# Attention's value step: sums' transposes behind the products, both ScalarE copies together, the latent keys' copy on ScalarE

## The chip, the cores and the metric

The kernel runs on one core of one Trainium2 chip. The metric is the device time of an execution in microseconds. TensorE multiplies and transposes into PSUM, VectorE, ScalarE and GpSimd do the rest, and SyncE mostly issues DMAs. Each engine works through its own queue in order and waits for the others by semaphores.

## The reference, cut to what matters

An encoder trunk of two layers over 1024 tokens of 1024 columns. A layer has a mixer with three groups of heads (6 gated DeltaNet heads, 6 grouped-query attention heads, 4 latent-attention heads), an output projection, and a mixture of experts. The change lies in the attention of the two softmax groups, 10 heads per layer, and in the keys of the latent one:

```python
def attend(q_blk):
    s = jnp.einsum('bhgqd,bhkd->bhgqk', q_blk, k) * scale
    p = jax.nn.softmax(s, axis=-1)
    return jnp.einsum('bhgqk,bhkd->bhgqd', p.astype(v.dtype), v)
...
kv = (rms_norm(ckv, kv_lat_gain) @ w_ukv).reshape(B, S, H, MLA_NOPE + MLA_V)
k_nope = rms_norm(kv[..., :MLA_NOPE], kn_gain)
v = kv[..., MLA_NOPE:]
```

## The kernel before

A layer runs in stages: input projection and the DeltaNet chunks' preparation, then one long attention stage (`attend`) into which the DeltaNet scan, the making of the latent heads' inputs (`mla_inputs`), the modulation products for later (`ada`) and the loading of the output weights are mixed, then output projection, routing and experts. Everything is written out in Python; a scheduler orders the instructions of each engine afterwards, so that the written order is only a start: a change of a few lines moves the neighbours too.

`attend` goes through 10 heads with 8 query blocks of 128 tokens. For a block, `scores` multiplies queries and keys into two PSUM tiles `s` of 128x512, VectorE takes the maximum (L1132, L1134), ScalarE the exponential with its row sums (L1137). At every second block VectorE adds the two halves of the row sums (L1142, tile `rs`, 128x2) and takes the reciprocal (L1143). `trans` transposes the probabilities on TensorE (L1157) and copies them to `pT`, one half on ScalarE (L1162), the other on VectorE (L1160).

`values` closes a pair of blocks; there are 80 such pairs in the two layers. It takes the one PSUM tile `pv` (a whole bank, one buffer) for two things. TensorE first spreads the reciprocals over 64 partitions by two transposes (L1171, into `rsb`, partitions 0 to 63), then does eight products (L1175) that fill partitions 0 to 63 with the even and 64 to 127 with the odd key tiles. ScalarE copies the odd half to `olo` (L1178), VectorE adds both halves to `o` (L1179), ScalarE copies `rsb` (L1182) to another buffer of the name `olo`, which has two, and GpSimd multiplies (L1183). The result goes to DRAM by a DMA on ScalarE's queue (L1186). The next pair's transposes have to wait until `pv` has been read.

In `mla_inputs`, `products` makes the latent heads' rows, 16 times in the two layers: a product of 128x512 in a PSUM tile `pt` holds keys and values of four heads. VectorE copies the keys to `mK` (L584), ScalarE the values to `mV` (L585), both out of this one tile.

GpSimd works all through the stage, for `ada` (L123, L125), for the scan and for the DeltaNet output (L917, L930).

Of the kernel before, what the change touches and what calls it, by code (L numbers as in the profile page):

```python
# [8 lines left out]
FT = mybir.dt.float32  # L9
FR = mybir.dt.float32r  # L10
I32 = mybir.dt.int32
AF = mybir.ActivationFunctionType
OP = mybir.AluOpType
# [16 lines left out]
class Trunk:  # L30
# [497 lines left out]
    def mla_inputs(self, l, mx, tp, wk):  # L528

        nc, I = self.nc, self.I  # L530
# [38 lines left out]
        def products(lat, t, Q, K, V):  # L569
            ps = self.pt_p.tile([128, 4, 128], FT, name="pt")  # L570
            nc.tensor.transpose(ps[:, 0, :], lat[:, t, 0:128], self.ident)
            nc.tensor.transpose(ps[0:64, 1, :], lat[:, t, 128:192], self.ident)
            nc.tensor.transpose(ps[:, 2, :], lat[:, t, 192:320], self.ident)
            ct = wk.tile([128, 3, 128], FT, name="ct")
            for j, n in ((0, 128), (1, 64), (2, 128)):
                nc.scalar.activation(ct[0:n, j, :], ps[0:n, j, :], AF.Copy, scale=gq[0:n, j:j + 1])
            yield
            pq = self.pt_p.tile([128, 4, 128], FT, name="pt")
            pqv = pq.rearrange("p a b -> p (a b)")[:, 0:384]
            self._prod(nc, pqv, [(ct[:, 0, :], wuq[:, 0, :]), (ct[0:64, 1, :], wuq[0:64, 1, :])])  # L580
            nc.scalar.activation(Q[:, t].rearrange("p a b -> p (a b)"), pqv, AF.Copy)
            pk = self.pt_p.tile([128, 4, 128], FT, name="pt")
            nc.tensor.matmul(pk.rearrange("p a b -> p (a b)"), ct[:, 2, :], wukv, start=True, stop=True)
            nc.vector.tensor_copy(K[:, t, :, 0:64], pk[:, :, 0:64])  # L584
            nc.scalar.activation(V[:, t], pk[:, :, 64:128], AF.Copy)  # L585

        lat = latent(0)
# [1 line left out]
        for c in range(4):  # L589
# [4 lines left out]
            K = wk.tile([128, hn, 4, 96], FT, name="mK", bufs=self.QB)  # L594
# [4 lines left out]
            for _ in products(cur, 0, Q, K, V):  # L599
                yield  # L600
            if c < 3:
                lat = latent(c + 1)
            for _ in products(cur, 1, Q, K, V):
                yield
# [490 lines left out]
    def attend(self, mx, heads, aside):  # L1095
        nc = self.nc
        seq = [(hd, qt) for hd in heads for qt in range(NT)]
        ops, gens, P, PT = {}, {}, {}, {}
        self.dn_done, self.att_over, turn = False, False, {"s": 0, "p": 0, "v": 0}

        def bank(which):

            if self.dn_done:
                turn[which] += 1
                if turn[which] % self.TM[which] in self.TB[which]:
                    return self.dps.tile([128, 512], FT, name="dn")
            return {"s": self.s_p, "p": self.pt_p, "v": self.pv_p}[which].tile([128, 512], FT, name={"s": "s", "p": "pt", "v": "pv"}[which])

        def scores(u):
            (h, prep, row, scale), qt = seq[u]  # L1110
            if u == 0:
                gens[h] = prep()
                next(gens[h])
                ops[h] = next(gens[h])
            if u // NT + 1 < len(heads):
                h1, p1 = heads[u // NT + 1][:2]
                if qt == 0:
                    gens[h1] = p1()
                    next(gens[h1])
                if qt == self.QP:  # L1120
                    ops[h1] = next(gens[h1])
            passes = ops[h][0]
            i = u % 2
            if i == 0:
                self.su = self.wp.tile([128, 4], FT, name="su", bufs=3)
            su = self.su
            sm = self.wp.tile([128, 4], FT, name="sm", bufs=6)
            ss = []
            for kf in range(2):
                s = bank("s")  # L1130
                self._prod(nc, s, [(q[:, qt * 128:qt * 128 + 128], k[:, kf * 512:kf * 512 + 512]) for q, k in passes])
                nc.vector.tensor_reduce(sm[:, kf:kf + 1], s, axis=AX.X, op=OP.max)  # L1132
                ss.append(s)
            nc.vector.tensor_scalar(sm[:, 2:3], sm[:, 0:1], sm[:, 1:2], -scale, op0=OP.max, op1=OP.mult)  # L1134
            p = self.wp.tile([128, NT, 128], FT, name="P", bufs=self.PB)
            for kf in range(2):
                nc.scalar.activation(p[:, 4 * kf:4 * kf + 4].rearrange("p a b -> p (a b)"), ss[kf], AF.Exp, bias=sm[:, 2:3], scale=scale,  # L1137
                                     accum_out=su[:, 2 * kf + i:2 * kf + i + 1])
            rs = None
            if i:  # L1140
                rs = self.wp.tile([128, 2], FT, name="rs", bufs=3)
                nc.vector.tensor_tensor(rs, su[:, 0:2], su[:, 2:4], op=OP.add)  # L1142
                nc.vector.reciprocal(rs, rs)  # L1143
            P[u] = p, rs

        def trans(u):
            p, rs = P.pop(u)
            i = u % 2
            if i == 0:
                PT[u // 2] = (self.wp.tile([128, NT, 256], FT, name="pT"),)  # L1150
            pT = PT[u // 2][0]
            if i:
                PT[u // 2] += (rs,)
            for hf in range(2):
                ps = bank("p").rearrange("p (a b) -> p a b", a=4)
                for k in range(4):
                    nc.tensor.transpose(ps[:, k, :], p[:, hf * 4 + k, :], self.ident)  # L1157
                o = (slice(None), slice(hf * 4, hf * 4 + 4), slice(i * 128, i * 128 + 128))
                if hf:
                    nc.vector.tensor_copy(pT[o], ps)  # L1160
                else:
                    nc.scalar.activation(pT[o], ps, AF.Copy)  # L1162

        def values(w):
            (h, _, row, _), qt = seq[2 * w]
            V = ops[h][1]
            pT, rs = PT.pop(w)
            both = bank("v").rearrange("p (a b) -> p a b", a=2)
            pv, rsb = both[:, 0], both[0:64, 1]
            for i in range(2):  # L1170
                nc.tensor.transpose(rsb[:, i * 128:i * 128 + 128], rs[:, i:i + 1].to_broadcast([128, 64]), self.ident)  # L1171

            for k in range(NT):
                hs = slice(64 * (k % 2), 64 * (k % 2) + 64)
                self.pe_last = nc.tensor.matmul(pv[hs], V[:, k, :], pT[:, k, :], start=(k < 2), stop=(k >= NT - 2), tile_position=(0, hs.start))  # L1175
            o = self.wp.tile([64, 256], FT, name="o")
            lo = self.wp.tile([64, 256], FT, name="olo")
            nc.scalar.activation(lo, pv[64:128], AF.Copy)  # L1178
            nc.vector.tensor_tensor(o, pv[0:64], lo, op=OP.add)  # L1179
            if self.OM:  # L1180
                rr = self.wp.tile([64, 256], FT, name="olo")
                nc.scalar.activation(rr, rsb, AF.Copy)  # L1182
                nc.gpsimd.tensor_tensor(o, o, rr, op=OP.mult)  # L1183
            else:
                nc.vector.tensor_tensor(o, o, rsb, op=OP.mult)
            self.qa.dma_start(mx["oT"][qt // 2][row:row + 64], o)  # L1186

        n = len(seq)
        la = self.LA
        for u in range(la):  # L1190
            scores(u)
        for u in range(n):
            if self.VF and (u - self.VL) % 2 == 0 and u >= self.VL + 1:
                values((u - self.VL - 1) // 2)
            if u + la < n:
                scores(u + la)
            trans(u)
            if not self.VF and (u - self.VL) % 2 == 1 and u >= self.VL + 1:
                values((u - self.VL - 1) // 2)
            next(aside, None)  # L1200
        for w in sorted(PT):
            values(w)
        self.att_over = True
        for _ in aside:
            pass
        self.pe_last = None
# [678 lines left out]
```

## Time and profile before

| | |
|---|---|
| median of 3 runs | 2909.56 us (2903.85 to 2910.96) |
| the profiled execution's own time | 2897.23 us |
| its span, first to last instruction | 2895.4 us |
| mean granted clock of TensorE | 0.911 of full |
| TensorE, VectorE, ScalarE, GpSimd busy | 2443.4, 1971.0, 1365.3, 1414.9 us |
| attention stage of layer 0 | about 438 to 960 us |
| attention stage of layer 1 | about 1866 to 2356 us |

The profile is of one execution. Its rows name engines PE (TensorE), PEld (its weight load), DVE (VectorE), ACT (ScalarE), POOL (GpSimd) and SP (SyncE). A row's "x80" counts instructions, three numbers behind it are the shortest, the median and the longest in ns, and "waits" are idle times of an engine with the instruction that ended them.

### The profile page before, as it was taken

To read this page: it belongs to the slowest core of one execution; us is meant where nothing else is said; L and a number is where in the kernel's file an instruction comes from. 1 tells how busy PE (TensorE), PEld (TensorE's weight loads), DVE (VectorE), ACT (ScalarE), POOL (GpSimd) and SP (SyncE) were. 2 spreads that over 40 slices of the span, in tenths; PEclk is the share of its full clock that TensorE was granted. 3 is DMA by queue.
4 is the path that set the end of the run, shared out by engine and by line. 5 is a ranking of instruction groups with operands and counts; after the bars stand their busy time and mean duration, and the time that the engine had idled before them with its cause. 6 is when DMAs were issued, how large, how long until landed. Compare 5 with 4: busy or idle time off the path is not lost. (4 is left out here: it accounts for less than half of the span.)

```text
span 2895.4 us, 46986 instructions
## 1 busy us (share of the span) xinstructions
PE 2443.4 (84%) x16804; PEld 1834.1 (63%) x16804; DVE 1971.0 (68%) x3424; ACT 1365.3 (47%) x2500; POOL 1414.9 (49%) x1425
## 2 busy tenths in 40 slices
PE   4978976988699968999959879779888999699986
PEld 4866864656467856765548768646565678566543
DVE  5596779587777467676625867795967754866654
ACT  4436335654466225455454263356565742345543
POOL 2874766455667233234337837663656412332432
PEclk9989978999799979999969889889998999799988
DMA  7435653686454647999754356537784445599994
GB/s 236 124 91 141 163 141 89 178 210 169 116 154 117 230 176 252 304 308 324 254 131 126 91 141 158 137 90 184 205 201 116 122 144 189 198 311 290 313 321 140
DMA packets 499532, 534.51 MB, mean 185 GB/s; under 512 B 252722, under 2 KB 421234, under 8 KB 490592
## 3 DMA queue, kind: packets, MB, share of 16 engines
q1 hardware_dynamic: 397408, 461.93, 52.4%
q0 software_dynamic: 19680, 33.61, 5.4%
q10 hardware_dynamic: 82208, 35.93, 4.9%
q8 instruction: 134, 2.20, 0.3%
q14 instruction: 102, 0.84, 0.1%
HBM read 436.03 MB, written 124.65 MB: 194 GB/s over the span
## 5 line engine op out<-in xcount | busy, mean ns | idle before, releaser
L1579 DVE TENSOR_TENSOR wlo<-w,whi 128x2048 fp32r<-128x2048 f32 x126 | 287.7, 2289 | 88.0 <-ACT whi L1576 82.8
L1576 ACT ACTIVATE whi<-w 128x2048 fp32r<-128x2048 f32 x130 | 247.6, 1911 | 118.7 <-PE up L219 99.4
L1137 ACT ACTIVATE P<-s,sm 128x512 f32<-128x512 f32 x294 | 199.2, 683 | 101.7 <-DVE sm L1134 58.3
L1132 DVE TENSOR_REDUCE sm<-s 128x1 f32<-128x512 f32 x294 | 198.5, 682 | 57.5 <-PE s L219 55.5
L123 POOL TENSOR_TENSOR ada_wt<-ada_wt,cs 128x512 f32<-128x512 f32 (+1 forms) x128 | 187.0, 1464 | 101.2 <-DMA ada_wt<-in_ada_w 100.0
L125 POOL TENSOR_TENSOR ada_wt<-ada_wt 128x256 f32<-128x256 f32 (+2 forms) x256 | 209.5, 826 | 5.4
L219 PE MATMUL acc<-whi,hhi 128*128 128x280 f32 x640 | 194.7, 315 | 10.0 <-ACT hhi L193 5.3
L1157 PE MATMUL pt<-ident,P 128*128 128x128 f32 x1136 | 181.4, 295 | 25.8 <-DVE qh L996 7.8
L219 PE MATMUL acc<-whi,hlo 128*128 128x280 f32 x640 | 198.7, 314 | 3.2 <-POOL hlo L196 3.2
L219 PE MATMUL acc<-wlo,hhi 128*128 128x280 f32 x640 | 195.6, 309 | 0.3 <-DVE wlo L212 0.2
L1175 PE MATMUL pv<-pT,vr 128*64 128x256 f32 x1280 | 184.5, 410 | 8.7 <-DVE pT L1160 5.5
L219 PE MATMUL s<-kh,qh 128*128 128x512 f32 (+1 forms) x294 | 148.1, 504 | 47.3 <-ACT P L1137 45.5
L1157 PEld LDWEIGHTS pt<-ident,P 128*128 128x128 f32 x1136 | 143.1, 151 | 66.5 <-issue 10.9
L1631 POOL DMA_INDIRECT xg<-xn,itok x75 | 112.2, 1496 | 149.3 <-PE xt L1647 99.5
L219 PE MATMUL y<-w,aT 128*128 128x512 f32 x360 | 166.9, 603 | 0.5 <-ACT aT L1683 0.5
L219 PE MATMUL up<-whi,hTh 128*128 128x512 f32 x360 | 152.8, 426 | 0.5 <-ACT hTh L1648 0.5
L219 PE MATMUL up<-wlo,hTh 128*128 128x512 f32 x360 | 146.0, 406 | 6.4 <-DVE wlo L1579 6.4
L219 PE MATMUL up<-whi,hTl 128*128 128x512 f32 x360 | 148.7, 413 | 0.0
L1183 POOL TENSOR_TENSOR o<-o,olo 64x256 f32<-64x256 f32 x80 | 59.2, 740 | 173.7 <-ACT olo L1182 158.2
L1175 PEld LDWEIGHTS pv<-pT,vr 128*64 128x64 f32 x1280 | 88.2, 144 | 77.4 <-issue 37.0
L219 PEld LDWEIGHTS acc<-whi,hhi 128*128 128x128 f32 x640 | 125.5, 200 | 17.3 <-ACT hhi L193 6.1
L219 PEld LDWEIGHTS acc<-whi,hlo 128*128 128x128 f32 x640 | 127.1, 199 | 9.3 <-POOL hlo L196 4.1
(480 smaller groups left out, 6901.3 us busy)
## 6 DMA issues: line engine op xcount, KB each, us to landing
w<-in_moe_w SPq DMA_DIRECT2D x260, 512.0 KB
w<-in_moe_w SPq DMA_DIRECT2D x65, 1024.0 KB
ada_wt<-in_ada_w SPq DMA_DIRECT2D x96, 256.0 KB
dg<-ch SPq DMA_DIRECT2D x64, 288.0 KB
ada_wt<-in_ada_w SPq DMA_DIRECT2D x32, 512.0 KB
ch<-aq SPq DMA_DIRECT2D x64, 192.0 KB
wraw<-in_w_in SPq DMA_DIRECT2D x32, 280.0 KB
qkr<-gqk ACTq DMA_DIRECT2D x32, 256.0 KB
```

Source lines behind the costliest of these rows:

```text
L123: eng.tensor_tensor(wt, wt, self.cs.unsqueeze(2).to_broadcast([128, KT, cols]), op=OP.mult)
L125: eng.tensor_tensor(wt[:, 0:n, :], wt[:, 0:n, :], wt[:, n:2 * n, :], op=OP.add)
L219: mm = nc.tensor.matmul(ps, a, b, start=(i == 0), stop=(i == n - 1))
L1132: nc.vector.tensor_reduce(sm[:, kf:kf + 1], s, axis=AX.X, op=OP.max)
L1137: nc.scalar.activation(p[:, 4 * kf:4 * kf + 4].rearrange("p a b -> p (a b)"), ss[kf], AF.Exp, bias=sm[:, 2:3], scale=scale, accum_out=su[: ...
L1157: nc.tensor.transpose(ps[:, k, :], p[:, hf * 4 + k, :], self.ident)
L1175: self.pe_last = nc.tensor.matmul(pv[hs], V[:, k, :], pT[:, k, :], start=(k < 2), stop=(k >= NT - 2), tile_position=(0, hs.start))
L1183: nc.gpsimd.tensor_tensor(o, o, rr, op=OP.mult)
L1576: c = nc.scalar.activation(hi, w, AF.Copy)
L1579: s = (nc.gpsimd if first is not None and first < self.HB - 1 else nc.vector).tensor_tensor(lo, w, hi.bitcast(FT), op=OP.subtract)
L1631: nc.gpsimd.indirect_dma_start(out=g[0:n], out_offset=None, in_=st["xn"], in_offset=bass.IndirectOffsetOnAxis(ap=it[0:n], axis=0), bounds_ ...
```

## The change

In `values` the two transposes of the reciprocals stand behind the eight products. ScalarE's two copies stand together, behind the products and ahead of VectorE's sum, and the second one has a tile name of its own, `orr`, with two buffers. GpSimd's multiplication is as before; the branch for a switch that was always on is gone. In `products` ScalarE copies the keys too. Behind the change L1173 are the products, L1175 the transposes, L1180 and L1181 the copies, L1182 the sum; L1183 is the multiplication in both.

```diff
@@ -581,7 +581,7 @@
             nc.scalar.activation(Q[:, t].rearrange("p a b -> p (a b)"), pqv, AF.Copy)
             pk = self.pt_p.tile([128, 4, 128], FT, name="pt")
             nc.tensor.matmul(pk.rearrange("p a b -> p (a b)"), ct[:, 2, :], wukv, start=True, stop=True)
-            nc.vector.tensor_copy(K[:, t, :, 0:64], pk[:, :, 0:64])
+            nc.scalar.activation(K[:, t, :, 0:64], pk[:, :, 0:64], AF.Copy)
             nc.scalar.activation(V[:, t], pk[:, :, 64:128], AF.Copy)
 
         lat = latent(0)
@@ -1167,22 +1167,20 @@
             pT, rs = PT.pop(w)
             both = bank("v").rearrange("p (a b) -> p a b", a=2)
             pv, rsb = both[:, 0], both[0:64, 1]
-            for i in range(2):
-                nc.tensor.transpose(rsb[:, i * 128:i * 128 + 128], rs[:, i:i + 1].to_broadcast([128, 64]), self.ident)
 
             for k in range(NT):
                 hs = slice(64 * (k % 2), 64 * (k % 2) + 64)
                 self.pe_last = nc.tensor.matmul(pv[hs], V[:, k, :], pT[:, k, :], start=(k < 2), stop=(k >= NT - 2), tile_position=(0, hs.start))
+            for i in range(2):
+                nc.tensor.transpose(rsb[:, i * 128:i * 128 + 128], rs[:, i:i + 1].to_broadcast([128, 64]), self.ident)
+
             o = self.wp.tile([64, 256], FT, name="o")
             lo = self.wp.tile([64, 256], FT, name="olo")
+            rr = self.wp.tile([64, 256], FT, name="orr")
             nc.scalar.activation(lo, pv[64:128], AF.Copy)
+            nc.scalar.activation(rr, rsb, AF.Copy)
             nc.vector.tensor_tensor(o, pv[0:64], lo, op=OP.add)
-            if self.OM:
-                rr = self.wp.tile([64, 256], FT, name="olo")
-                nc.scalar.activation(rr, rsb, AF.Copy)
-                nc.gpsimd.tensor_tensor(o, o, rr, op=OP.mult)
-            else:
-                nc.vector.tensor_tensor(o, o, rsb, op=OP.mult)
+            nc.gpsimd.tensor_tensor(o, o, rr, op=OP.mult)
             self.qa.dma_start(mx["oT"][qt // 2][row:row + 64], o)
 
         n = len(seq)
```

**ScalarE, layer 0, the first value step of the stage.** The words in brackets are the engines whose semaphores an instruction waits for; `gsq` and `lat` belong to the latent rows. Before:

```order
L1178 ACTIVATE olo<-pv 64x256 [waits PE_49]
L559 ACTIVATE gsq<-lat 128x704 [waits DMAHW6_49,DVE_49,Activation_49]
L1162 ACTIVATE pT<-pt 128x4x128 [waits PE_49]
L1182 ACTIVATE olo<-pv 64x256 [waits DVE_49]
L1137 ACTIVATE P,su<-s,sm 128x512 [waits DVE_49]
L1137 ACTIVATE P,su<-s,sm 128x512
```

With the change:

```order
L1180 ACTIVATE olo<-pv 64x256 [waits PE_49]
L1181 ACTIVATE orr<-pv 64x256
L559 ACTIVATE gsq<-lat 128x704 [waits DMAHW6_49,DVE_49,Activation_49]
L1162 ACTIVATE pT<-pt 128x4x128 [waits PE_49]
L1137 ACTIVATE P,su<-s,sm 128x512 [waits DVE_49]
L1137 ACTIVATE P,su<-s,sm 128x512
```

The second copy waits for VectorE no more and follows the first; so it is at all 80 pairs.

**ScalarE, layer 0, one of the 16 latent products.** `mQ`, `mK` and `mV` are the latent queries, keys and values, `x` belongs to the scan. Before:

```order
L883 ACTIVATE x<-dn 64x384 [waits DMAHW1_49,PE_49]
L1178 ACTIVATE olo<-pv 64x256 [waits PE_49]
L1182 ACTIVATE olo<-pv 64x256 [waits DVE_49]
L581 ACTIVATE mQ<-pt 128x384 [waits PE_49]
L1186 DMA oT_134<-o 64x256 [waits DMAHW0_49,Pool_49]
L585 ACTIVATE mV<-pt 128x256 [waits DVE_49]
L1137 ACTIVATE P,su<-s,sm 128x512 [waits Activation_49]
```

With the change:

```order
L883 ACTIVATE x<-dn 64x384 [waits PE_49]
L1184 DMA oT_134<-o 64x256 [waits DMAHW4_49,Pool_49]
L581 ACTIVATE mQ<-pt 128x384 [waits PE_49]
L584 ACTIVATE mK<-pt 128x4x64 [waits PE_49]
L585 ACTIVATE mV<-pt 128x256
L1137 ACTIVATE P,su<-s,sm 128x512 [waits DVE_49,Activation_49]
```

Keys and values are now copied one after the other with a wait for TensorE alone, and the value step's copies have gone elsewhere in the queue.

**TensorE, layer 0, the second value step.** `s` are scores, the products with `qkr` are the next head's transposes. Before:

```order
L1171 MATMUL pv<-ident,rs 64x128 x2
L1175 MATMUL pv<-pT,vr 64x256
L219 MATMUL s<-kh,qh 128x512
L219 MATMUL s<-kl,qh 128x512
L1175 MATMUL pv<-pT,vr 64x256 x3
L219 MATMUL s<-kh,qh 128x512
L219 MATMUL s<-kl,qh 128x512
L991 MATMUL pt<-ident,qkr 128x128 x4
L1175 MATMUL pv<-pT,vr 64x256 x4
L1157 MATMUL pt<-ident,P 128x128 x8
```

With the change:

```order
L1173 MATMUL pv<-pT,vr 64x256 x3
L219 MATMUL s<-kh,qh 128x512
L219 MATMUL s<-kl,qh 128x512
L1173 MATMUL pv<-pT,vr 64x256
L219 MATMUL s<-kh,qh 128x512
L219 MATMUL s<-kl,qh 128x512
L991 MATMUL pt<-ident,qkr 128x128 x4
L1173 MATMUL pv<-pT,vr 64x256 x4
L1175 MATMUL pv<-ident,rs 64x128 x2
L1157 MATMUL pt<-ident,P 128x128 x8
```

The transposes of the reciprocals went from the head of the step to its end; in between, the products are cut in other places by scores.

## Rows read from the trace of the kernel before

**Rows 1.** The page's part 1: busy time, share of the span and instructions of each engine.

```profile
PE 2443.4 (84%) x16804; PEld 1834.1 (63%) x16804; DVE 1971.0 (68%) x3424; ACT 1365.3 (47%) x2500; POOL 1414.9 (49%) x1425
```

**Rows 2.** Busy time in two attention stages; columns: stretch, length, then engines' busy time (instructions).

```profile
438.00:960.00 522.00, 436.23 (x3914) 309.77 (x3914) 381.57 (x783) 287.14 (x681) 302.04 (x332) 0.90 0.56 150
1866.00:2356.00 490.00, 414.82 (x3898) 296.84 (x3898) 365.90 (x799) 289.47 (x686) 247.98 (x294) 0.92 0.57 150
```

**Rows 3.** Who waits around tile olo (us, times): first the waiters for it, then reverse.

```profile
L1179 DVE TENSOR_TENSOR o<-pv,olo x80: 381/414/419, 454.1 to 2354.0; 64x256 f32<-64x256 f32 x80
L1182 ACT ACTIVATE olo<-pv x80: 358/377/379, 454.6 to 2354.5; 64x256 f32<-64x256 f32 x80
...
  ACT olo L1182: 158.2, 42
  DVE o L1179: 49.8, 33
...
  ACT olo L1178: 37.0, 22
...
  PE pv L1171: 14.6, 10
```

**Rows 4.** Line L585, ScalarE's copy of V, and tile mK's copy L584 on VectorE.

```profile
L585 ACT ACTIVATE mV<-pt x16: 378/383/384, 563.1 to 2104.7; 128x256 f32<-128x256 f32 x16
...
  DVE mK L584: 29.1, 13
...
L584 DVE COPY mK<-pt x16: 407/424/426, 562.6 to 2104.2; 128x256 f32<-128x256 f32 x16
```

**Rows 5.** Busy time in 46 stretches of ScalarE's waits at L1182 and L585, the sum.

```profile
sum 78.97, PE 52.11 PEld 35.41 DVE 75.58 ACT 0.13 POOL 52.65; mean PE 1.13 PEld 0.77 DVE 1.64 ACT 0.00 POOL 1.14
```

**Rows 6.** Timeline from 747 us; columns: start, length, engine, line, operation, idle before it.

```profile
747.38 3.86 POOL L917 TENSOR_TENSOR os<-os,ob 128x384 f32<-128x384 f32 x4
747.39 8.25 DVE L1142 TENSOR_TENSOR rs<-su 128x2 f32<-128x2 f32 x1 [0.92 <-ACT P L1137]
...
751.88 3.75 POOL L123 TENSOR_TENSOR ada_wt<-ada_wt,cs 128x1024 f32<-128x1024 f32 x2
```

**Rows 7.** The same view, 838 to 848 us.

```profile
838.17 7.49 DVE L1142 TENSOR_TENSOR rs<-su 128x2 f32<-128x2 f32 x1
...
846.36 0.41 DVE L1179 TENSOR_TENSOR o<-pv,olo 64x256 f32<-64x256 f32 x1
...
846.80 0.38 ACT L1182 ACTIVATE olo<-pv 64x256 f32<-64x256 f32 x1 [4.56 <-DVE o L1179]
...
847.23 0.44 PE L1171 MATMUL pv<-ident,rs 128*64 128x128 f32 x2 [1.61 <-ACT olo L1182]
```

**Rows 8.** Who waits for the reciprocals, tile rs; the addition L1142 in it.

```profile
L1142 DVE TENSOR_TENSOR rs<-su x80: 130/160/8248, 447.7 to 2344.7; 128x2 f32<-128x2 f32 x80
...
  PE pv L1171: 16.1, 6
```

**Rows 9.** Timeline, 2194 to 2218 us.

```profile
2194.17 1.08 PE L1175 MATMUL pv<-pT,vr 128*64 128x256 f32 x8
...
2215.91 0.38 ACT L1182 ACTIVATE olo<-pv 64x256 f32<-64x256 f32 x1 [5.17 <-DVE o L1179]
...
2216.99 0.20 DVE L1134 TENSOR_SCALAR sm<-sm 128x1 f32<-128x1 f32 x1
2217.22 0.69 ACT L1137 ACTIVATE P<-s,sm 128x512 f32<-128x512 f32 x1 [0.19 <-DVE sm L1134]
...
2218.06 0.79 PE L219 MATMUL s<-kh,qh 96*128 96x512 f32 x1 [6.66 <-ACT P L1137]
```

**Rows 10.** The addition L1142 in layer 0's attention stage, then in layer 1's.

```profile
L1142 DVE TENSOR_TENSOR rs<-su 128x2 f32<-128x2 f32 x40 | 40.0, 1000 | 15.4 <-ACT P L1137 15.2
...
L1142 DVE TENSOR_TENSOR rs<-su 128x2 f32<-128x2 f32 x40 | 11.7, 293 | 15.8 <-ACT P L1137 15.6
```

## The prediction

> **What bounds the kernel now.** I read the page first: TensorE is busy for 84% of the span, VectorE for 68%, ScalarE for 47% [rows 1]. No engine is the bound of the whole, so I asked for each engine's busy time by stage. The change touches only the two attention stages, 438 to 960 us and 1866 to 2356 us, 1012 us together [rows 2]. There TensorE is busy for 436.23 + 414.82 = 851.05 us and idle for 161 us; VectorE is busy for 747.47 us, 0.74 of the time; ScalarE for 576.6 us, 0.57. The reader should see that nobody is full there: the stages are a ring of queues kept in order (scores, maximum, exponential, transposes, copies, value products), and time is lost where the queues meet.
>
> The third view is the wait lists of the instructions that the change touches. ScalarE's copy of the sums' part (L1182) kept its engine idle for 49.8 us, 33 times, until VectorE's sum L1179 was done [rows 3], though it needs no number from it. In the latent part the copy of V (L585) waited 29.1 us, 13 times, for VectorE's copy of K out of the same PSUM tile [rows 4]. So ScalarE stands still for 78.97 us in 46 stretches because VectorE is late.
>
> The fourth view decides how much of that is worth anything: each engine's busy time in those 46 stretches, summed [rows 5]. Of the 78.97 us, VectorE is busy for 75.58 (96%) and TensorE for 52.11. So VectorE isn't waiting for ScalarE there, it is what everybody waits for, and TensorE idles in 26.9 us of it.
>
> The fifth view, the timeline, says why VectorE is late. At 747.39 the sum of two row sums (L1142, 128x2, median 160 ns) takes 8.25 us, from GpSimd's first product at 747.38 until the pair of products that begins at 751.88 has ended at 755.63; at 838.17 it takes 7.49 us, and ScalarE's stall of 4.56 us before 846.80 is its tail [rows 6, 7]. All 80 of these take 40.0 + 11.7 = 51.7 us [rows 10] instead of 80 x 0.16 = 12.8 [rows 8], so some 39 us go into them.
>
> **The change part by part.** The sum is made against the profiled execution, 2897.23 us (span 2895.4 us and 1.8 around it). The median of the runs shown is 2909.56, 12.33 above it (0.4%); I take that offset over.
>
> (a) *K's copy moves to ScalarE.* VectorE loses 16 copies of 0.42 us, 6.7 us [rows 4]. Weighted with its busy share in the stages that is 6.7 x 0.74 = 5.0 us. ScalarE gains 16 copies; the same shape for V takes 0.383 us there [rows 4], so 6.1 us, on an engine idle for 435 us of the 1012, which also loses the 29.1 us of stalls: nothing. Should ScalarE be the late engine where a head's latents are made, the 6.1 us would stand on the path.
>
> (b) *ScalarE no longer stops for VectorE.* All 96 waits are gone from the order. The gain lies between nothing and the 26.9 us in which TensorE idled in the stalls. I take a tenth, 2.7 us, because the row that shows a whole case shows next to none: after the stall of 5.17 us before 2215.91 the exponential starts at 2217.22, right behind the maximum that VectorE ends at 2217.19, and TensorE's wait of 6.66 us ends with that exponential [rows 9]. Without the stall the exponential could not have started earlier.
>
> (c) *The bank is freed one step earlier.* The products' tile has one PSUM buffer. TensorE's next value step waited 14.6 us, 10 times, for L1182, its last reader [rows 3]. At 847.23 it starts 0.41 us after the sum's end at 846.77 [rows 7]. Now the sum is the last reader: 10 x 0.41 = 4.1 us.
>
> (d) *The transposes go behind the products.* They need the reciprocal of the row sums, and TensorE waited 16.1 us for it, 6 times, with the products queued behind [rows 8]. Now the products go first. The gain lies between 0 and 16.1 us. I take the first four of eight products, half of 1.08 us [rows 9], at each of the 6: 3.2 us, since products five to eight need VectorE's own half of the transposed probabilities, which is late when the reciprocal is. The transposes cost the same as before; the products end 0.38 us earlier for it, so the first copy doesn't start later.
>
> (e) *The sum now comes behind both copies.* VectorE waited 37.0 us, 22 times, for the first copy [rows 3]; each such wait grows by the second copy, 0.377 us: 22 x 0.37 = 8.1 us, weighted 0.74: 6.0 us lost. Below: nothing, if the sum's place in the queue moves as well. Above: both copy and transposes at full price, 22 x 0.75 = 16.5 us. Behind a waiting sum stand maxima and copies of probabilities, and ScalarE's exponentials wait for those. The wait itself follows from the rows: L1182 stood waiting for a sum that it shares only the bank with, so the reverse order waits as well. [...] Were only data waited for, (e) would be nought and the sum 15.0 us of gain.
>
> (f) *A tile of its own for the reciprocals* costs 2 KB a partition and takes one tie to GpSimd's multiplication away. GpSimd's waits for L1182 (158.2 us) [rows 3] become waits for the sum, 0.41 us earlier; the output's DMA follows the multiplication as before. Nothing. No transfer is added or taken away on any queue; the scheduler shifts them with their neighbours.
>
> Sum: -5.0 - 2.7 - 4.1 - 3.2 + 6.0 = **-9.0 us**, that is 2888.2 for the profiled execution and 2909.56 - 9.0 = **2900.6** for the median.
>
> **The rivals.**
>
> *VectorE stays late and nothing else counts.* Then ScalarE's stall only moves to its next wait for VectorE's maximum; (b), (c) and (d) fall away and -5.0 + 6.0 = +1.0 us remain: **2910.6**. For it speak the 96% of rows 5 and the case of rows 9; against it that TensorE's waits in (c) and (d) are its own, with products ready.
>
> *A worse meeting with GpSimd.* The change re-sorts every queue in the two stages, and so the moments at which L1142 meets a train of GpSimd products. Mechanism: an addition that starts just as such a train starts waits for its end, and maximum and copies wait behind it. Price: the same 40 additions took 40.0 us in layer 0 and 11.7 in layer 1 [rows 10]. If layer 1 comes to look like layer 0, VectorE loses 28.3 us, weighted 0.74: 20.9, and -9.0 + 20.9 = +11.9 us: **2921.5**. It decides from 9.0/0.74 = 12.2 us more in L1142. [...]
>
> *The ring turns freely.* If TensorE gets back all it idled in the stalls, -26.9 - 5.0 - 4.1 + 6.0 = -30.0 us: **2879.6**. The meeting of the rival before, the other way round, gives nearly the same (-9.0 - 20.9). For it: 161 us of TensorE's idle time and 79 us of a wait without need. Against: rows 5.
>
> *It doesn't do what it says.* The order shows both copies together without a wait between at all 80 places, so 1 in 50; **2909.6**.
>
> **How the numbers follow.** A measurement of this kernel can tell about 0.3%, 8.7 us, from no change. Chances: my forecast 0.36, VectorE late 0.27, worse meeting 0.19, free ring 0.16, nothing done 0.02. The forecast itself lies close to the bound: of its 0.36, 0.26 go to faster, 0.08 to same, 0.02 to slower. VectorE late: 0.02, 0.21, 0.04. Worse meeting: 0, 0.03, 0.16. Free ring: all faster; nothing done: same. Together 0.44 faster, 0.34 same, 0.22 slower. The low end takes TensorE's 26.9 us and VectorE's 6.7 us whole and charges nothing: 2876.0. The high end takes (e) at its upper bound with nothing gained, 16.5 us: 2926.1; the four times worked out lie inside.
>
> **What would show it.** In the profile after: ScalarE's waits for the sum and for K's copy gone (79 us to 0); VectorE's wait in front of the sum up from 37 us to some 45; the wait for the reciprocal gone from in front of the value step and no equal wait for transposed probabilities in its place; TensorE idle in the two stages down from 161 us by about 9. If L1142 adds up to far more or less than 51.7 us, the meeting with GpSimd has decided. I am wrong if TensorE's idle time in the two stages doesn't fall, or if the stages outside them change by more than the attention stages do.

## The result, and the profile after

The changed kernel takes **2873.68 us** (median of 6 executions, 2861.89 to 2886.54); the kernel before took 2902.47 in the same session (2896.19 to 2910.96). The ratio is **0.9898, interval 0.9865 to 0.9931**: the medians lie 28.8 us apart. The same changed kernel, measured a second time, gave 2882.81 against 2896.96, 14.2 us apart, ratio 0.9936 [0.9906, 0.9966]. (A ratio here can differ from the quotient of the two medians, in this case 0.995, by some 0.2%.) Forecast were -9.0 us and a range down to 2876.0; of the 26.9 us between the forecast 2900.6 and 2873.68, 7.1 are the kernel before's own median, which was 2909.56 when the forecast was made.

The profiled execution of the changed kernel took 2886.54 us (span 2884.7), the slowest of its six, while the one of before was near its fastest. So the two traces differ by 10.7 us, not 28.8, and I profiled each kernel once more. The seven lines below are the changed kernel's stages in the view of stretches (columns as in [rows 2]): layer 0's attention, its output projection, its experts, layer 1's preparation, then layer 1's attention, output projection and experts.

```profile
435.90:918.10 482.20, 404.96 (x3843) 291.44 (x3840) 366.80 (x767) 285.85 (x684) 292.26 (x323) 0.92 0.58 151
918.10:1040.50 122.40, 113.29 (x572) 96.38 (x571) 50.19 (x63) 28.44 (x48) 31.77 (x18) 0.92 0.61 202
1040.50:1457.10 416.60, 354.13 (x1505) 229.42 (x1505) 279.98 (x344) 187.56 (x221) 136.44 (x95) 0.91 0.84 271
1457.10:1857.30 400.20, 341.75 (x2469) 297.82 (x2471) 275.45 (x504) 177.29 (x301) 268.14 (x309) 0.87 0.53 138
1857.30:2345.60 488.30, 407.63 (x3806) 290.05 (x3803) 353.17 (x763) 286.80 (x684) 230.77 (x266) 0.91 0.52 135
2345.60:2449.70 104.10, 102.30 (x546) 87.68 (x544) 48.87 (x63) 28.24 (x48) 22.37 (x8) 0.99 0.66 223
2449.70:2884.70 435.00, 368.03 (x1546) 240.32 (x1546) 286.75 (x347) 189.60 (x221) 164.02 (x97) 0.91 0.81 262
```

The same view of the kernel before, its stages cut at the same instructions:

```profile
438.60:947.30 508.70, 422.93 (x3848) 298.73 (x3845) 376.87 (x776) 283.51 (x676) 300.82 (x331) 0.90 0.55 145
947.30:1056.00 108.70, 106.70 (x572) 91.39 (x570) 49.10 (x64) 28.23 (x48) 22.40 (x10) 1.00 0.65 218
1056.00:1475.70 419.70, 355.40 (x1504) 231.12 (x1504) 280.72 (x343) 187.84 (x222) 141.21 (x95) 0.90 0.82 269
1475.70:1887.60 411.90, 342.38 (x2467) 298.02 (x2469) 277.09 (x504) 179.70 (x302) 271.30 (x308) 0.87 0.52 134
1887.60:2354.90 467.30, 401.74 (x3807) 286.55 (x3804) 348.61 (x771) 283.62 (x676) 231.99 (x266) 0.93 0.56 146
2354.90:2459.20 104.30, 102.36 (x547) 87.73 (x545) 48.17 (x62) 28.22 (x48) 22.51 (x8) 1.00 0.59 201
2459.20:2895.40 436.20, 367.11 (x1546) 239.06 (x1546) 286.87 (x347) 189.28 (x221) 158.78 (x97) 0.91 0.81 261
```

With the second profile of each (lengths in us; a kernel further down whose profiled execution was much slower than its others, as the kernel before with the output work from step 42 was, at 2961.16 us against a median of 2934.80, is not compared by stages):

| stage | before | before, again | after | after, again | means' difference |
|---|---|---|---|---|---|
| up to attention 0 | 438.6 | 441.9 | 435.9 | 437.9 | -3.4 |
| attention 0 | 508.7 | 500.2 | 482.2 | 479.5 | **-23.6** |
| output projection 0 | 108.7 | 108.5 | 122.4 | 122.1 | **+13.7** |
| experts 0 | 419.7 | 427.5 | 416.6 | 417.4 | -6.6 |
| preparation 1 | 411.9 | 415.1 | 400.2 | 397.2 | **-14.8** |
| attention 1 | 467.3 | 471.5 | 488.3 | 480.3 | **+14.9** |
| output projection 1 | 104.3 | 104.3 | 104.1 | 104.1 | -0.2 |
| experts 1 | 436.2 | 420.0 | 435.0 | 435.7 | +7.3 |

Three things stand out. The two attention stages together give -23.6 + 14.9 = **-8.7 us**, the size of the forecast's sum. But four stages move by some 14 us or more, and two of them, outside attention, hold nothing that the change touches. And all stages together give -12.7 us, -4.0 of them outside attention: that is close to the 14.2 us of the second measurement, while the rest of the first one's 28.8 us stands in no profile, so what made it stays open.

Of the waits that the prediction named, these are the answers to [rows 3], the views of tiles orr and olo:

```profile
L1181 ACT ACTIVATE orr<-pv x80: 370/377/380, 451.4 to 2344.6; 64x256 f32<-64x256 f32 x80
...
  DVE o L1182: 167.6, 40
...
  DVE o L1182: 21.5, 16
```

```profile
L1180 ACT ACTIVATE olo<-pv x80: 380/381/384, 451.0 to 2344.2; 64x256 f32<-64x256 f32 x80
L1182 DVE TENSOR_TENSOR o<-pv,olo x80: 395/406/418, 452.8 to 2345.1; 64x256 f32<-64x256 f32 x80
...
  PE pv L1175: 46.3, 40
  ACT orr L1181: 21.5, 16
...
  PE pv L1173: 1.8, 2
```

In these lists 167.6 us is GpSimd's wait for the sum and 46.3 us ScalarE's for TensorE. ScalarE no longer waits for the sum (49.8 us before); its first copy waits for TensorE alone. VectorE's sum waits 21.5 us, 16 times, for the second copy, where it waited 37.0 us for the first [rows 3]. TensorE's wait for the bank is 1.8 us instead of 14.6, and nobody on TensorE waits for a reciprocal any more. K's copy waits 8.5 us for TensorE and V's copy for nothing (29.1 us before [rows 4]).

Where those waits went, the lists of waits of each attention stage tell (us in total, times, longest). Before, attention 0 and then, as the last two lines, attention 1:

```profile
PE pv L1171 <- DVE rs L1143: 11.9, 4, 7.6
PE pv L1171 <- ACT olo L1182: 11.1, 6, 2.7
...
PE pt L1157 <- ACT pT L1162: 4.3, 2, 2.3
...
ACT P L1137 <- DVE sm L1134: 41.1, 24, 8.0
...
PE pv L1171 <- DVE rs L1143: 4.1, 2, 2.3
...
ACT P L1137 <- DVE sm L1134: 25.5, 22, 3.5
```

After, in the same order:

```profile
PE pt L1157 <- DVE pT L1160: 10.9, 2, 10.1
...
PE pt L1157 <- ACT pT L1162: 4.1, 3, 2.7
...
ACT P L1137 <- DVE sm L1134: 50.8, 32, 9.6
...
PE pv L1173 <- DVE pT L1160: 4.4, 3, 1.9
...
ACT P L1137 <- DVE sm L1134: 52.2, 30, 7.2
```

TensorE's 23.0 us ahead of the value step of layer 0 are gone. 10.9 come back, nearly all in one wait, where the next transposes of probabilities (L1157) wait for VectorE's copy of the last ones (9.8 in the second profile). ScalarE waits 103.0 us for VectorE's maximum instead of 66.6 (87.5 instead of 67.3 in the second profiles): 79 us of stalls went, and its waits at the next meeting with VectorE grew by 36 (20). L1142 changed by 2.8 us in all, 34.8 + 19.7 us against the 51.7 of [rows 10], so the meeting with GpSimd did not decide.

The output projection of layer 0 is new. This is its timeline in the changed kernel (columns as in [rows 6]):

```profile
925.27 0.39 PE L219 MATMUL oacc<-owl,oh 128*128 128x512 f32 x1
...
926.51 4.82 POOL L125 TENSOR_TENSOR ada_wt<-ada_wt 128x512 f32<-128x512 f32 x4
...
931.29 0.86 POOL L126 TENSOR_TENSOR ada_acc<-ada_wt 128x128 f32<-128x128 f32 x2
...
932.20 2.08 PE L94 MATMUL pt<-ones,ada_acc 128*64 128x1 f32 x16 [6.54 <-POOL ada_acc L126]
...
935.92 0.63 PE L219 MATMUL oacc<-owh,ol 128*128 128x512 f32 x1
...
939.99 0.39 PE L219 MATMUL oacc<-owl,oh 128*128 128x512 f32 x1
```

Attention is over sooner, but GpSimd's sums for the next layer's modulation (`ada`, dealt out to the attention steps) are not. TensorE waits 6.54 us for them, and then its products take 0.63 us instead of 0.39 until 939.75: in 932.2 to 939.8 the granted clock is 0.51, from 939.8 to 1035.3 it is 1.00. Of the stage's +13.7 us 7.1 are idle time and 6.6 longer products (113.29 us against 106.70, 572 products each). No run shows how much of the 6.6 follows from the wait, and not all of it can: the view of stretches gives a granted clock of 0.50 from 919.24 to 922.65, ahead of the wait, from 929.48, within it, to 939.72, and from 1035.30 to the stage's end; the same stage of the kernel before has 1.00.

### The profile page after: what moved, and what is told of

It reads as the page before. It is cut to its first block, busy times and chain, and to the rows that moved or that the text cites. A ratio compares the mean times of both kernels' runs of the same rounds, so it can differ in the third digit from the quotient of the medians.

```text
span 2884.7 us, 47012 instructions
## 1 busy us (share of the span) xinstructions
PE 2438.2 (85%) x16804; PEld 1835.6 (64%) x16804; DVE 1967.2 (68%) x3408; ACT 1369.0 (47%) x2514; POOL 1410.4 (49%) x1425
## 5 line engine op out<-in xcount | busy, mean ns | idle before, releaser
L1157 PE MATMUL pt<-ident,P 128*128 128x128 f32 x1136 | 182.3, 295 | 44.0 <-DVE pT L1160 13.8
L125 POOL TENSOR_TENSOR ada_wt<-ada_wt 128x256 f32<-128x256 f32 (+2 forms) x256 | 216.3, 853 | 4.9
L1157 PEld LDWEIGHTS pt<-ident,P 128*128 128x128 f32 x1136 | 144.7, 152 | 80.2 <-DVE pT L1160 16.7
L1173 PE MATMUL pv<-pT,vr 128*64 128x256 f32 x1280 | 178.4, 408 | 10.8 <-DVE pT L1160 6.8
L1183 POOL TENSOR_TENSOR o<-o,orr 64x256 f32<-64x256 f32 x80 | 57.9, 723 | 184.1 <-DVE o L1182 167.6
L1173 PEld LDWEIGHTS pv<-pT,vr 128*64 128x64 f32 x1280 | 87.7, 143 | 76.8 <-issue 28.9
L219 PEld LDWEIGHTS acc<-whi,hlo 128*128 128x128 f32 x640 | 126.4, 198 | 12.4 <-POOL hlo L196 7.7
L219 PEld LDWEIGHTS acc<-whi,hhi 128*128 128x128 f32 x640 | 124.9, 199 | 13.7 <-ACT hhi L193 6.1
```

Source lines behind the costliest of these rows:

```text
L125: eng.tensor_tensor(wt[:, 0:n, :], wt[:, 0:n, :], wt[:, n:2 * n, :], op=OP.add)
L219: mm = nc.tensor.matmul(ps, a, b, start=(i == 0), stop=(i == n - 1))
```

## The experiments

The first four groups ask which part of the change makes the time; the later ones, begun when those gave no answer, ask whether any part does. In all diffs the first file is the kernel before, unless said.

**The parts of the change alone.** K's copy on ScalarE, nothing else:

```
-            nc.vector.tensor_copy(K[:, t, :, 0:64], pk[:, :, 0:64])
+            nc.scalar.activation(K[:, t, :, 0:64], pk[:, :, 0:64], AF.Copy)
```

> The kernel before with the latent keys' copy on ScalarE alone. Theory W (ScalarE's needless waits for VectorE are the gain, in proportion to the 29.1 of 79 us of waits that go here): 10 to 12 us faster, ratio about 0.996, ScalarE's wait in front of the copy of V gone, and layer 0's attention stage shorter by half of that. Theory G (the re-sorted queues meet GpSimd differently): no relation to the waits; time moves with what the addition L1142 takes in all (51.7 us before), within 10 us either way. Theory V (VectorE's relief counts): 16 copies of 0.42 us, 3 to 6 us faster, ratio 0.998 to 0.999.

Measured: 1.0048 [1.0016, 1.0079]. The 29.1 us of ScalarE's waits are gone and the time is 0.5% longer. The whole value step, with K's copy left on VectorE (the changed kernel with the edit above undone):

> The changed kernel with the latent keys' copy back on VectorE: the value step's part alone. Theory W: 49.8 of 79 us of waits gone, so 16 to 20 us faster, ratio about 0.994, and with the keys alone the two add up to the whole change's 29 us. Theory G: no such addition; the sum of the two single parts misses the whole by 10 us or more. Theory V: same as before within 3 us, as VectorE has the same work.

Measured: 0.9921 [0.9892, 0.9949]; attention 0 takes 479.0 us, attention 1 476.5, the output projection 112.5, the preparation of layer 1 410.6. So the value step seemed to hold the whole gain. Its parts alone:

```
-            for i in range(2):
-                nc.tensor.transpose(rsb[...], rs[...], self.ident)
             for k in range(NT):
                 ...
+            for i in range(2):
+                nc.tensor.transpose(rsb[...], rs[...], self.ident)
```

> Of the value step's part only the order on TensorE: products first, transposes of the reciprocals behind; the sum still stands between the two copies. If TensorE's wait for the reciprocals was what cost time, layer 0's attention stage is 10 to 16 us shorter, ratio 0.994 to 0.997, and with the copies alone the two add up to the value step's 23 us. If ScalarE's wait was it, that wait stays at some 50 us and the ratio is 0.998 to 1.003.

Measured: 0.9997 [0.9965, 1.0028], although the waits for the reciprocals are gone and ScalarE's wait for the sum falls to 20.7 us. Copies together, in two tiles, with the transposes still ahead:

```
             nc.scalar.activation(lo, pv[64:128], AF.Copy)
+            nc.scalar.activation(rr, rsb, AF.Copy)
             nc.vector.tensor_tensor(o, pv[0:64], lo, op=OP.add)
...
-                nc.scalar.activation(rr, rsb, AF.Copy)
```

> Of the value step's part only the copies: both together with a tile each, then the sum; the transposes stay ahead of the products, the latent keys stay on VectorE. If ScalarE's wait for the sum (49.8 us) is what cost time, layer 0's attention stage is 20 to 30 us shorter than the 508.7 before and the time 15 to 23 us less, ratio 0.992 to 0.995. If TensorE's wait for the reciprocals (16.1 us) was it, layer 0's stage is within 8 us of before and the ratio 0.998 to 1.002.

Measured: 1.0009 [0.9964, 1.0055]; TensorE still waits 16.1 us for the reciprocals. The second tile alone (`olo` to `orr` at L1181):

> The kernel before with the second copy in a tile name of its own and nothing else: every wait of ScalarE for VectorE stays, but the scheduler sorts the queues anew. If waits decide: same, within 4 us, ratio 0.998 to 1.002, each attention stage within 8 us of before. If any new sorting moves this kernel, a stage changes by 10 us or more either way, as layer 1's did by plus 9 to plus 21 us in all four kernels run so far.

Measured: 0.9979 [0.9944, 1.0015]. And the transposes behind with the second tile, the sum still between the copies:

> The kernel before, with the transposes of the sums behind the products and the reciprocals' copy in a tile of its own, but the sum still between the two copies and K's copy on VectorE: the value step of the change without its copies together. It tells which pair makes the gain of 0.8% that the whole value step has (ratio 0.992) and that transposes alone (0.9997) and copies together with the own tile (1.0009) do not have. Theory (the gain needs the copies together and the transposes behind the products, since with the sum between them ScalarE still stands waiting for VectorE): ratio 0.997 to 1.001, layer 0's attention stage 495 to 505 us, ScalarE's waits for the sum near 15 to 20 us. Rival (the own tile with the transposes behind is enough, the order of copies and sum does not matter): ratio 0.990 to 0.994, layer 0's attention stage 480 to 485 us.

Measured: 0.998 [0.9956, 1.0003]. No part alone, nor that pair, moves the time by more than 0.2%; only all of them together did. That can be an interaction, or chance in how the queues are sorted.

**The same kernels once more.** The changed kernel again, and a second profile of the kernel before:

> The changed kernel once more, for a second profile and for the times of the same chip: ratio 0.987 to 0.993. Theory W: ScalarE's waits are gone again and layer 0's attention stage is again some 25 us shorter than before; layer 1's, which was 21 us longer in the first profile, comes out anywhere between minus 5 and plus 21 us, if that was the accident of one execution; theory G says it is 15 to 21 us longer again, as the order in layer 1 is then the cause.

> The kernel before once more, for a second profile: if layer 1's attention stage of 467.3 us belongs to this order, it comes out within 8 us of that, and layer 0's within 8 us of 508.7; if the stages' lengths are accidents of an execution, they differ by 10 us or more.

Measured: 0.9936 [0.9906, 0.9966] and 2890.84 us; the stages are in the table above. Attention, preparation and output projection repeat within 8.5 us. The experts of one and the same kernel differ by up to 16.2 us between two executions, with nothing changed in them.

**K's wait without K's move.** V's copy written ahead of K's, K's still on VectorE:

```
-            nc.vector.tensor_copy(K[:, t, :, 0:64], pk[:, :, 0:64])
             nc.scalar.activation(V[:, t], pk[:, :, 64:128], AF.Copy)
+            nc.vector.tensor_copy(K[:, t, :, 0:64], pk[:, :, 0:64])
```

> The kernel before, with the copy of V written ahead of the copy of K where a head's latents are made: ScalarE no longer waits for VectorE's copy out of the same tile, but K's copy stays on VectorE. Theory (what the move of K's copy costs, ratio 1.005 alone, is ScalarE's added work and the re-sorted queues, the removed wait is worth next to nothing): ratio 0.998 to 1.002. Rival (the removed wait of 29.1 us is worth time, and ScalarE's added copies eat it): ratio below 0.997.

Measured: 1.0017 [0.9992, 1.0043]. The wait is gone from ScalarE, VectorE waits 7.0 us for V's copy, and TensorE's transposes, which never waited for K's copy before, now wait 7.1 us for it. Nothing is gained.

**L1142 without its second SBUF input.** The changed kernel, and later the kernel before, with

```
-                nc.vector.tensor_tensor(rs, su[:, 0:2], su[:, 2:4], op=OP.add)
+                nc.vector.tensor_reduce(rs, su.rearrange("p (k i) -> p i k", k=2), axis=AX.X, op=OP.add)
```

> The changed kernel with the addition L1142 written as a sum over one input (a reduction over pairs) in place of an addition of two, so that VectorE doesn't read two SBUF inputs there. If the addition is long because GpSimd holds it up, its 80 instances take under 20 us in place of 54, VectorE's waits behind it go, and the kernel is 15 to 30 us faster than the changed one, ratio to before 0.980 to 0.985; if another cause makes it long, it stays at about 50 us and the time at the changed kernel's, 0.990. Theory W alone says 0.990.

> The kernel before, with the sum of the two row sums as a reduction of one input in SBUF, so that GpSimd's products do not hold it up: its 51.7 us fall to some 12. Theory (the hold-up stands on the path with VectorE's busy share, 0.74 of 39 us): ratio 0.988 to 0.993. Rival (what VectorE gains there goes into its other waits, as in the changed kernel, where the same edit moved nothing): 0.997 to 1.002. As a partner of the changed kernel with the same edit (0.9941) it gives a fourth pair.

Measured: 0.9941 [0.9909, 0.9972] on the changed kernel (no gain over it) and 0.9929 [0.9899, 0.996] on the kernel before. The hold-up itself goes with the edit: line L1142 in the changed kernel, and then in the changed kernel with the edit (durations in ns, min/median/max):

```profile
L1142 DVE TENSOR_TENSOR rs<-su x80: 143/161/9756, 445.1 to 2335.3; 128x2 f32<-128x2 f32 x80
```

```profile
L1142 DVE TENSOR_REDUCE rs<-su x80: 140/156/158, 450.3 to 2332.5; 128x2 f32<-128x4 f32 x80
```

**The late modulation.** The changed kernel with the modulation dealt out faster (`AR` from 0.5 to 0.65 units a step):

> The changed kernel, with the pace at which the next layer's modulation (ada) is dealt out to the attention steps raised from 0.5 to 0.65 units a step, so that its GpSimd sums are done before attention ends. Theory (the shorter attention stage of layer 0 gives some 13 us back in the output projection, because the modulation's sums on GpSimd are late there): the wait of TensorE for ada_acc at the head of layer 0's output projection (6.5 us) goes and that stage falls from 122 to about 109 us; if nothing is paid for it inside attention, the time falls by about 10 us against the changed kernel, to a ratio of about 0.987 to the kernel before. Rival (the modulation's work is only moved into attention, where GpSimd and VectorE meet): the output projection falls to 109 us, but layer 0's attention stage grows from 480 to 490 us or more, and the ratio stays between 0.990 and 0.994.

Measured: 0.9991 [0.9972, 1.0011]. The output projection is back to 106.0 us, with no wait for GpSimd in it:

```profile
437.40:936.10 498.70, 411.55 (x3864) 296.42 (x3861) 361.80 (x770) 287.06 (x684) 300.28 (x332) 0.91 0.56 149
936.10:1042.10 106.00, 105.08 (x553) 90.33 (x552) 48.96 (x62) 28.23 (x48) 22.41 (x8) 0.99 0.66 219
```

But attention 0 takes 498.7 us instead of 481, the preparation of layer 1 411.7 instead of 399, and the whole gain of the change is gone, though its value step and its copies are all in place. The rival, that the work only moves into attention, has it right, and worse.

**Pairs: the change on other pacings.** If the mechanics make the gain, the change must show it under another pacing too. The partner of the last run is the kernel before with the same pace:

> The kernel before, with the modulation dealt out at 0.65 units a step instead of 0.5: the partner of the changed kernel with that pace (0.9991). Theory (mechanics: the value step is worth some 0.8 to 1.0% under any pacing, and the faster pace costs some 0.7% in either kernel): ratio to the kernel before 1.005 to 1.011, layer 0's attention stage longer than 510 us. Rival (order: the gain belongs to one interleaving): ratio 0.997 to 1.003, layer 0's attention stage 495 to 510 us.

Measured: **0.9921 [0.989, 0.9952]**, faster by as much as the value step was, without it. A second pair begins the delta net's output and the output weights at step 42 instead of 36 (`D0`):

> The kernel before, with the delta net's output and the output weights begun at step 42 instead of 36: a second pacing of the side work. No theory says how it stands to the kernel before (0.99 to 1.01); what counts is the changed kernel with the same pacing beside it.

> The changed kernel, with the delta net's output and the output weights begun at step 42 instead of 36. Theory (mechanics): its ratio to the kernel before lies 0.008 to 0.011 below that of the kernel before with the same pacing. Rival (order): the two ratios differ by less than 0.003, or the other way round.

Measured: 1.011 [1.0074, 1.0145] and 0.9988 [0.996, 1.0016]. A third begins the modulation at step 26 instead of 32 (`A0`):

> The kernel before, with the modulation begun at step 26 instead of 32, at the old pace: a third pacing of the side work. It is the partner of the changed kernel with the same; alone it may lie anywhere from 0.99 to 1.01.

> The changed kernel, with the modulation begun at step 26 instead of 32. Theory now (the mechanics are worth the some 10 us of the forecast on average, 0.3 to 0.5%, and each re-sorting of the queues adds a shift of up to 1% of either sign): the ratio within the pair lies between 0.985 and 1.007; with layer 0's attention stage shorter than its partner's by 10 to 25 us, since that has been so in every pair, and the rest of the difference elsewhere. Rival (the mechanics are worth nothing): layer 0's attention stage no shorter than its partner's.

Measured: 0.9975 [0.9949, 1.0002] and 0.9969 [0.9936, 1.0001]. All pairs, the ratio within a pair worked out from the two:

| both kernels with | changed : before | attention 0 | attention 1 | both |
|---|---|---|---|---|
| nothing else (means of two) | 0.990, 0.994 | -23.6 us | +14.9 us | -8.7 us |
| modulation at 0.65 | 1.007 | -15.3 | +7.8 | -7.5 |
| output work from step 42 | 0.988 | (not compared) | (not compared) | |
| modulation from step 26 | 0.999 | -19.4 | +2.8 | -16.6 |
| one-input L1142 | 1.001 | -13.6 | +5.5 | -8.1 |

The mean of the five ratios, the plain one as 0.992, is 0.9975, 7 us of gain; single pairs scatter around it by 0.008 (standard deviation), 22 us, so the mean is uncertain by 0.003. In time, the change's own worth can't be told from nothing, nor from the -9.0 forecast. Inside the two attention stages the sign is steady: 7.5 to 16.6 us shorter in all four pairs, layer 0 shorter and layer 1 longer each time. That is no proof of the size, for other single profiles move the same two stages as far from the mean of the kernel before (973.9 us): the second tile alone by -7.6 us, the one-input L1142 by -18.5, the transposes alone by -19.3 at a ratio of 0.9997, the modulation at 0.65 by +10.9.

**Both edits that gained without the change.** The kernel before with the modulation at 0.65 and the one-input L1142:

> The kernel before, with both edits: the modulation at 0.65 units a step (0.9921 alone) and the one-input sum of row sums. If the two add up, 0.983 to 0.988, faster than the changed kernel; if the sum's edit only re-sorts the queues again, anywhere from 0.988 to 1.000.

Measured: 1.0002 [0.9973, 1.0031] (the quotient of the medians is 0.998). Two edits worth 0.8% and 0.7% alone give next to nothing together. No version ran that is faster than the changed kernel beyond the uncertainty; the kernel before with either of these edits equals it.

**What moves, then?** The preparation of layer 1 shows it best, since nothing in it was edited. Its middle 100 us in the view of stretches: before, then the changed kernel, then the kernel before with the modulation at 0.65, then the changed kernel with that:

```profile
1625.70:1725.70 100.00, 83.90 (x380) 69.33 (x378) 70.75 (x115) 49.21 (x74) 47.87 (x44) 0.83 0.44 114
```

```profile
1607.10:1707.10 100.00, 88.10 (x456) 73.49 (x454) 82.53 (x131) 53.66 (x85) 59.60 (x52) 0.90 0.53 139
```

```profile
1628.20:1728.20 100.00, 88.08 (x457) 73.55 (x455) 81.83 (x127) 53.65 (x85) 59.62 (x52) 0.90 0.51 134
```

```profile
1615.20:1715.20 100.00, 80.66 (x364) 66.30 (x364) 68.37 (x113) 49.99 (x75) 45.83 (x46) 0.83 0.42 108
```

TensorE does 456 and 457 products there in the second and third, 380 and 364 in the first and last. TensorE's instructions in this stage stand in the same order, row by row, in the changed kernel and in the kernel before at the faster pace; the kernel before and the one with the one-input L1142 share another order. The stage takes 400.2, 397.2 and 399.2 us in the first order, 411.9, 415.1 and 412.0 in the second. The profiles with other orders give 407.3 to 420.0 us. So these some 14 us go with an order that the scheduler also finds without the change. They go with it only roughly: the kernel before with K's copy on ScalarE and the one with the copies together also share an order of TensorE's instructions here, row by row, and take 408.3 and 417.1 us.

## Why the prediction was wrong

**The step that failed is what was put at nothing: the re-sorting of the queues.** The prediction knew of it: part (f) said of the transfers that "the scheduler shifts them with their neighbours", and a rival priced what it does to L1142. Outside that rival it got no microsecond, in the sum or in the range. The runs put it at some 14 us for a single stage, of either sign (output projection 0 +13.7, preparation 1 -14.8), and at 0.8 to 1.1% for the whole kernel when a pacing number alone is changed (0.9921, 1.011). The range would have had to carry it beside the terms (the pairs scatter by 22 us); its low end of 2876.0 was made of two attention terms only, and the changed kernel's median lies 2.3 us below (that of the second measurement, 2882.81, lies inside). Both of the prediction's own conditions for being wrong were met: single stages outside attention changed by -14.8 and +13.7 us against -8.7 for the two attention stages, and TensorE's idle time in the two did not fall.

**The sum's -9.0 against -8.7 is luck.** Its terms are waits, so TensorE's idle time was to pay them. That is 150.4 us in the two stages before and 151.0 after (means of two profiles); what fell is TensorE's busy time, by 9.3 us for the same products. So it is in the pairs: idle time +15.7 us (modulation at 0.65), -4.2 (from step 26) and -1.9 (one-input L1142), busy time -23.2, -12.4 and -6.2.

**(a) K's copy, -5.0: not confirmed.** Alone it cost 0.5%, on top of the value step it changed nothing (0.9921 without, 0.990 and 0.994 with it). That is within what re-sorting does, so its own worth stays open.

**(b) ScalarE's stop, -2.7 of at most 26.9: the reading held.** Removing V's wait alone gave 1.0017 (with 7.1 us of TensorE's waits in exchange), and ScalarE's waits for VectorE's maximum grew in every pair: by 36 and 20 us here, 58.6 with the modulation at 0.65, 33.4 from step 26, 29.4 with the one-input L1142. Rows 5 had said so: who waits for the engine that all wait for gains little by waiting elsewhere. To that extent the rival "VectorE stays late" is right.

**(c) and (d), -4.1 and -3.2: the mechanism right in layer 0.** In attention 0, 23.0 us of TensorE's waits ahead of the value step went and 10.9 came back at VectorE's half of the probabilities, the late partner that (d) named, though the next transposes wait for it and not the products. TensorE's idle time in that stage fell in all four pairs, by 8.6 (plain, means), 1.3, 8.2 and 10.4 us. What no term had is that its busy time fell too, by 15.0, 14.0, 11.2 and 3.2 us for the same products. The granted clock of the stage rose in the first three, from 0.90 in both profiles to 0.92 and 0.91, from 0.89 to 0.91 and from 0.91 to 0.93; in the last it fell, from 0.93 to 0.91. Why, no run takes apart. In layer 1 there was little to gain (7.7 us at L1171) and the stage became longer in every pair, by 2.8 to 14.9 us. Why it does is not settled: ScalarE's wait for the maximum doubles there, from 25.5 to 52.2 us (44.2 in the second profile), but no run takes that apart from the order of the queues.

**(e) The sum behind both copies, +6.0: the loss did not come.** The wait was to grow from 37 to 45 us; it fell to 21.5 (22.7 in the second profile). It fell in two other pairs too (38.7 to 26.4 from step 26, 41.4 to 25.5 with the one-input L1142) and grew only with the modulation at 0.65, from 29.1 to 36.4. Whether the sum's place in VectorE's queue moved, the case that (e) had kept as its lower bound, no view here tells. The sum does wait for a copy of which it needs no number and with which it shares only the bank (21.5 us, 16 times), as L1182 had waited for the sum (49.8 us, 33 times). That each wait would grow by a whole second copy was the author's estimate, which no run shows by itself.

**The rivals.** The worse meeting with GpSimd did not come (54.5 us in L1142 against 51.7). Its mechanism is real: with L1142 as a reduction of one SBUF input the longest of the 80 takes 158 ns instead of 9756 in the changed kernel, and 158 instead of 8248 in the kernel before. Those 9.76 us began at 734.53, within a train of GpSimd products (from 731.92), and ended at 744.29, the train at 744.26. Whether the number of inputs or the other operation does that, no run takes apart. Its price was not real: taking it away gave 0.7% on the kernel before, nothing on the changed one and a loss of 0.8% at the faster pace. The free ring's 2879.6 is the nearest number to the result, but for the wrong reason: TensorE's idle time in the two stages, 151.3 and 149.4 us before, is 157.9 and 144.0 after.

## What to carry to other kernels

Where a scheduler sorts the queues again after every edit, one run of an edit measures the edit plus one draw of the order: here some 0.8%, more than the edit. Before a gain of that size is put down to a mechanism, run the pair under two or three other settings that should not matter, and the neutral settings by themselves; read the mechanism in its own stage and in its own quantity, here TensorE's idle time: a stage's length can agree with a forecast whose waits did not change in sum. And give the range of a prediction a term for the draw.

## What the runs showed that was not expected

Work that was hidden behind attention (GpSimd's modulation sums) can stand on the path when attention gets shorter (not always: with K's copy left on VectorE attention 0 is as short, 479.0 us, and the output projection takes 112.5 us instead of 122.4). In the changed kernel it costs 6.54 us of waiting, and the 7.6 us behind the wait pass at a granted clock of 0.51 (0.63 us a product instead of 0.39). Doing that work earlier ended this cost but won no time: at the pace of 0.65 attention 0 took 498.7 us instead of some 481, and begun at step 26 it left attention 0 at 481.1 and the output projection at 105.1, while the preparation of layer 1 took 414.0 instead of some 399.

Three profiles of two different kernels with the same order of TensorE's instructions agree within 3 us in a 400 us stage, and three with another order lie some 14 us above: the order of the queues goes with this kernel's time as its instructions do, though another pair of kernels with one order lies 8.8 us apart. In the experts' stages two executions of the kernel before differ by 7.8 and 16.2 us with no difference in the program (those of the changed kernel by under 1 us).
